# RWKV layer of a hybrid decoder: PSUM banks by size of product, key work in three staggered parts, bonus as four column tiles

## The chip, the cores and the metric

The kernel runs on one core of a Trainium2 chip. The metric is the device time of one execution in microseconds. TensorE (PE in the rows; PEld is its weight load) multiplies, VectorE (DVE) and ScalarE (ACT) work elementwise and empty PSUM, GpSimd (POOL) works elementwise in SBUF, SyncE (SP) issues most of the DMAs.

## The reference, cut to what matters

The model has two layers, one of sparse attention and one of RWKV-7 time mixing, each with a squared-ReLU MLP. The change is in the RWKV layer, for 256 tokens, 1024 features and 16 heads of 64:

```python
r, k, v = xr @ w_rkv[0], xk @ w_rkv[1], xv @ w_rkv[2]
decay = exp(-exp(w_log))
a = sigmoid(a0 + (xa @ a1) @ a2)
kk = k * k_k / |k * k_k|
kh = k * (1 + (a - 1) * k_a)
state = state * decay + (state @ -kk) * (kk * a) + v * kh     # one step per token
y = state @ r
y = groupnorm(y) * ln_w + ln_b + sum(r * kh * r_k) * v        # the last term is the bonus
out = (y * g) @ w_out
```

The kernel computes the recurrence in chunks of 64 tokens: inside a chunk the steps become products of matrices, with the inverse of a triangular matrix for each head and chunk, and a state goes from chunk to chunk.

## The kernel before

All weights come as chunks of 128 x 1024 (`wchunk`, from L227): SyncE loads a chunk into one of 4 buffers (wst), ScalarE rounds it (wh, L230), VectorE takes what the rounding left (wl, L232), with 5 buffers of each, and TensorE multiplies three times (L266 to L268). PSUM has two rings of four banks: `pmm` takes the next of the ring "mm", `pacc` the next of "acc". A tile waits until the tile that had its bank four allocations before is done with.

The RWKV layer runs, in the order of the program: receptance features (`feature_tile`, 8 of them), then for each of four pairs of feature tiles p and p + 4 the two key features (`keys_of`), and behind those of the next pair the key work of the pair (`key_pair`): the product pa for a with its tanh (th), the product pc with the exponentials E and Ei of the decay, the squares sq, on VectorE the products that fill AR and BK, the norms pn, the low blocks pL (LB and LO, the triangular parts, emptied by ScalarE at L986 to L989), on GpSimd F, kh in kk[:, 2:], the other half of BK, and r * kh (L1003), from which the bonus product pb (L1007) is made. Feature tiles use mm, everything in `key_pair` uses acc. Then the value product (`gemm_b`, 96 matmuls into acc) follows; its evacuation vt is also copied by DMA to VS. Then come, for chunks c, `products(c)` (pM, M; masked on GpSimd at L1073 for chunks 0 and 1, "late", and on VectorE at L1071 for 2 and 3), the gate products (pg), the key rows (pKB), and the gate steps on GpSimd (L1108 to L1111, on vt, bon, g and rowt).

The inverse stands behind that in the program: VectorE transposes and scales LB (L1123, L1124), then runs a loop of 31 steps, 116 instructions (L1130, L1133), transposes the result to T and TT (L1135, L1136); TensorE forms pU and pT (L1147, L1154) with copies T (L1149) and TT (L1156). A list of steps then runs over the chunks: Z right sides, Q solve with TT, S next state, M products, B key rows, Y output, N norm.

The order on every engine except SyncE is fixed when the kernel is built: a planner with a model of time goes through ready instructions, earlier ones of the program first. On the chip an engine keeps that order and waits. `issue_after(x)` puts the instructions that follow behind x on the engine of x; `first` (L1149) is such a mark for the chunks of the output weight. Larger tiles (`big`) take numbered slots from a free list and give them back with `done`.

Of the kernel before, what the change touches and what calls it, by code (L numbers as in the profile page):

```python
# [9 lines left out]
F32 = mybir.dt.float32  # L10
# [6 lines left out]
D = 1024  # L17
# [20 lines left out]
NSA_ORDER = ("K a0 h0 h1 l2 q0 q1 q2 q3 h2 G l3 T0 s0 a1 h3 s1 w0 H q4 q5 q6 q7 w1 "  # L38
             "C0 T1 s2 C1 s3 s4 P0 v0 v1 w2 P1 v2 s5 w3 s6 w4 v3 w5 v4 v5 w6 s7 v6 w7 v7").split()
LAG = 2  # L40
TAIL = 4
# [17 lines left out]
def _consts():  # L59
# [31 lines left out]
    mR = (s_ <= t_).astype(np.float32)  # L91
    parts["mmask"] = np.concatenate([mA, mR], 1).astype(np.float32)
    parts["par"] = np.stack([p < 64, p >= 64], 1).astype(np.float32)
    off, o = {}, 0
# [80 lines left out]
def trunk(ctx: ExitStack, tc: tile.TileContext, wb, x_in, wg, cw1k, cw1v, cw2, vecs_in, l1, w2, a2, g2, rows,  # L175
# [671 lines left out]
    def rwkv(inp):  # L847
        hn, dx, xrh, xrl, w2t, a2t, lo = inp
        with ExitStack() as es:
# [10 lines left out]

            rk2 = pool.tile([128, KT, 2], F32, name="rk2")
            P.tensor_tensor(rk2, cc("par")[:, None, :].to_broadcast([128, KT, 2]),
                            vec[:, V_RK * KT:V_RK * KT + KT][:, :, None].to_broadcast([128, KT, 2]), op=ALU.mult)
# [34 lines left out]
            def feature_tile(hT, lT, dst):  # L898

                wh, wl = wchunk("p (k c) -> p k c", k=8)  # L900
                p = pmm([128, S], "pa")
                for k in range(KT):
                    mm3(p, wh[:, k], wl[:, k], kt(hT, k), kt(lT, k), k == 0, k == KT - 1)
                act(dst, p, AF.Copy)
# [20 lines left out]
            bon = pool.tile([128, NT, H], F32, name="bon")  # L925
            bon4 = bon.rearrange("p t (i k s) -> p t i k s", i=2, k=4)
            F = pool.tile([128, NCH - 1, KT], F32, name="F")
# [17 lines left out]

            def key_pair(p, kk):

                ks_ = (p, p + 4)
                AR[p], BK[p] = big([128, 2, NCH, 2, C], f"AR{p}"), big([128, 2, NCH, 2, C], f"BK{p}")
                ar, bk = AR[p], BK[p]  # L950
                th = sm.tile([128, 2, S], F32, tag="th", bufs=2, name="th")
                th1 = sm.tile([128, 2, S], F32, tag="th1", bufs=2, name="th1")
                sq = sm.tile([128, 2, S], F32, tag="sq", bufs=2, name="sq")
                e_ = big([128, 2, NCH, C + 1], f"E{p}")
                Ei = big([128, 2, NCH, C + 1], f"Ei{p}")
                pa = pacc("pa2", [128, 2, S])
                for i, k in enumerate(ks_):
                    mm(pa[:, i], a2t[:, k * 128:(k + 1) * 128], aT, start=True, stop=True)
                for i, k in enumerate(ks_):
                    act(th[:, i], pa[:, i], AF.Tanh, scale=0.5, bias=hk[:, 0, k:k + 1])  # L960

                for i, k in enumerate(ks_):
                    pc = pacc("pc", [128, NT, 2, C + 1])
                    for t in range(NT):
                        mm(pc[:, t].rearrange("p c t -> p (c t)"), ld[t][:, k * 128:(k + 1) * 128], cen, start=True, stop=True)
                    act(e_[:, i], pc.rearrange("p a c t -> p (a c) t"), AF.Exp)
                    act(Ei[:, i], pc.rearrange("p a c t -> p (a c) t"), AF.Exp, scale=-1.0)
                for i, k in enumerate(ks_):
                    act(sq[:, i], kk[:, i], AF.Square, scale=vcol(V_KK, k))
                V.scalar_tensor_tensor(th1, th, 1.0, kk[:, :2], op0=ALU.add, op1=ALU.mult)  # L970
                for i, k in enumerate(ks_):
                    V.scalar_tensor_tensor(ar[:, i, :, 0], four(kk[:, i]), vcol(V_KK, k), e_[:, i, :, :C], op0=ALU.mult, op1=ALU.mult)
                    V.scalar_tensor_tensor(bk[:, i, :, i], four(th1[:, i]), vcol(V_KK, k), Ei[:, i, :, 1:], op0=ALU.mult, op1=ALU.mult)

                pn = pacc("pn", [128, NCH, 2])
                for c in range(NCH):
                    for i, k in enumerate(ks_):
                        mm(pn[rows_of(k), c], sq[:, i, c * C:(c + 1) * C], par, start=True, stop=True)
                pl = [pacc("pL", [128, NCH, C]) for _ in range(2)]
                for c in range(NCH):  # L980
                    for s in range(2):
                        for k in ks_:
                            mm(pl[s][rows_of(k), c], head(BK, k, s, c)[:, k // 4], head(AR, k, s, c)[:, 0], start=True, stop=True)
                for s in range(2):
                    lb, lo_ = [a.rearrange("p (c k s) t -> p c k s t", c=NCH, k=4)[:, :, p, s] for a in (LB, LO)]
                    act(lb, pl[s][:, :, :32], AF.Copy)  # L986
                    for r2 in r2s:
                        act(lb[r2], pl[s][r2, :, 32:], AF.Copy)
                    act(lo_, pl[s][:, :, 32:], AF.Copy)  # L989
                V.tensor_scalar(rn4[:, :, p], pn, 1e-24, -2.0, op0=ALU.max, op1=ALU.mult)  # L990
                for i, k in enumerate(ks_):
                    V.tensor_scalar(th[:, i], th[:, i], hk[:, 1, k:k + 1], hk[:, 2, k:k + 1], op0=ALU.mult, op1=ALU.add)
                P.tensor_tensor(kk[:, 2:], kk[:, :2], th, op=ALU.mult)
                for i in range(2):
                    P.tensor_tensor(bk[:, i, :, 1 - i], four(kk[:, 2 + i]), Ei[:, i, :, 1:], op=ALU.mult)

                    P.tensor_tensor(F[:, :, ks_[i]], e_[:, i, :NCH - 1, C], Ei[:, i, 1:, 0], op=ALU.mult)

                r2_ = pair_of(rr, p)
                V.tensor_tensor(ar.rearrange("p i c a t -> p (i c) a t")[:, :, 1], r2_.rearrange("p i (c t) -> p (i c) t", c=NCH),  # L1000
                                e_.rearrange("p i c t -> p (i c) t")[:, :, 1:], op=ALU.mult)

                P.tensor_tensor(kk[:, 2:], r2_, kk[:, 2:], op=ALU.mult)  # L1003
                pb = pacc("pb", [128, NT, 2, 2])
                for t in range(NT):
                    for i, k in enumerate(ks_):
                        mm(pb[:, t, i], kk[:, 2 + i, t * 128:(t + 1) * 128], rk2[:, k], start=True, stop=True)  # L1007
                act(bon4[:, :, :, p], pb, AF.Copy)
                done(e_, Ei, kk)


            kp = []

            def keys_of(p):
                kp.append(big([128, 4, S], f"kk{p}"))
                for i in range(2):
                    feature_tile(xkh, xkl, kp[p][:, i])
            keys_of(0)
            for p in range(1, 5):
                if p < 4:  # L1020
                    keys_of(p)
                if p == 3:
                    done(xkh, xkl)
                key_pair(p - 1, kp[p - 1])
            done(ld, a2t, rr)
            V.reciprocal(rn, rn)
            V.transpose(rnB, rn)

            Tb = big([128, 32, 32], "Tb")
            P.memset(Tb, 0.0)  # L1030
            dg = Tb.rearrange("p a b -> p (a b)")
            act(bass.AP(tensor=dg.tensor, offset=dg.offset, ap=[dg.ap[0], [33, 32]]), rnB, AF.Copy)

            sms.close()
            sm = es.enter_context(tc.tile_pool(name="rw2", bufs=1))
            Lb = big([128, 32, 32], "Lb")
            pd = big([128, 32, 32], "pd")
            T1 = big([128, 32, 32], "T1")
            vt = [big([128, D], f"vt{t}") for t in range(NT)]
            TT = sm.tile([128, 32, C], F32, name="TT")  # L1040
            for r2 in r2s:
                P.memset(TT[r2, :, :32], 0.0)
            VS = [big([128, H, DH], f"VS{c}") for c in range(NCH)]

# [6 lines left out]

            gemm_b(lambda k, sl: kt(xvh, k)[:, sl], lambda k, sl: kt(xvl, k)[:, sl], v_evac, D)
            done(xvh, xvl)


# [62 lines left out]
            key_rows(1)  # L1118
            gates(0)
            gates(1)  # L1120


            V.transpose(Lb.rearrange("p s t -> p t s"), LB.rearrange("p h t -> p t h"))  # L1123
            V.tensor_tensor(Lb, Lb, rnB[:, None, :].to_broadcast([128, 32, 32]), op=ALU.mult)  # L1124
            done(LB)
            for i in range(31):
                n, m_ = i + 1, 31 - i
# [15 lines left out]
            for bl in jb:  # L1143
# [4 lines left out]
                for p, r2 in zip(pU, r2s):  # L1148
                    first = act(T1[r2, bl], p[r2], AF.Copy)  # L1149
            for bl in jb:  # L1150
# [4 lines left out]
                for p, r1 in zip(pT, r1s):  # L1155
                    V.tensor_copy(TT[r1, bl, 32:], p[r1])  # L1156
            done(T1, LO)
# [115 lines left out]

            for o in "Z0 M2 Q0 S0 Z1 M3 B2 Q1 S1 Z2 Y0 Q2 S2 N0 Z3 Q3 Y1".split():
                if o[0] == "N":
# [79 lines left out]
```

## Time and profile before

| | us |
|---|---|
| median of 3 runs (767.73 to 768.32) | 767.97 |
| the profiled execution | 772.3 |
| its span | 770.5 |
| TensorE busy in the span | 732.2 (95%) |
| VectorE busy | 460.5 (60%) |
| ScalarE busy | 424.2 (55%) |
| GpSimd busy | 75.4 (10%) |
| mean granted clock of TensorE, as a share of 2.4 GHz | 0.969 |

Times in the rows are microseconds from the start of the span. Matmuls are pipelined: a row's time is longer than the distance to the next. The buffer numbers are left out of the names, so pa stands for the feature product and, at L958, for the product pa2, and th for th and th1; halves of an fp32 product are instructions of their own.

### The profile page before, as it was taken

To read this page: it belongs to the slowest core of one execution; us is meant where nothing else is said; L and a number is where in the kernel's file an instruction comes from. 1 tells how busy PE (TensorE), PEld (TensorE's weight loads), DVE (VectorE), ACT (ScalarE), POOL (GpSimd) and SP (SyncE) were. 2 spreads that over 40 slices of the span, in tenths; PEclk is the share of its full clock that TensorE was granted. 3 is DMA by queue.
4 is the path that set the end of the run, shared out by engine and by line. 5 is a ranking of instruction groups with operands and counts; after the bars stand their busy time and mean duration, and the time that the engine had idled before them with its cause. 6 is when DMAs were issued, how large, how long until landed. Compare 5 with 4: busy or idle time off the path is not lost. (4 is left out here: it accounts for less than half of the span.)

```text
span 770.5 us, 13414 instructions
## 1 busy us (share of the span) xinstructions
PE 732.2 (95%) x5292; PEld 627.9 (81%) x5292; DVE 460.5 (60%) x939; ACT 424.2 (55%) x830; POOL 75.4 (10%) x78
## 2 busy tenths in 40 slices
PE   7999999999999999999999669988899999999996
PEld 5876866789999899988899558678789899898995
DVE  5766798358455544578746469264765644555453
ACT  6626587347555655563657422565536655556562
POOL 1000000000000000001004550770110000000000
PEclk9999999999999999999999659979999999999999
DMA  8946200219655555680154102332214755555531
GB/s 286 324 137 249 81 31 6 81 55 316 187 188 188 189 184 180 214 273 1 62 185 138 55 0 90 92 103 83 87 51 137 234 186 187 188 191 191 189 114 54
DMA packets 32012, 111.50 MB, mean 145 GB/s; under 512 B 3629, under 2 KB 4141, under 8 KB 31950
## 3 DMA queue, kind: packets, MB, share of 16 engines
q1 hardware_dynamic: 30878, 108.94, 42.7%
q10 hardware_dynamic: 928, 1.19, 0.7%
q8 instruction: 41, 0.67, 0.4%
q0 software_dynamic: 144, 0.52, 0.2%
q14 instruction: 21, 0.17, 0.1%
HBM read 108.54 MB, written 1.05 MB: 142 GB/s over the span
## 5 line engine op out<-in xcount | busy, mean ns | idle before, releaser
L232 DVE TENSOR_TENSOR wl<-wst,wh 128x1024 fp32r<-128x1024 f32 x175 | 216.8, 1244 | 181.2 <-ACT wh L230 179.3
L230 ACT ACTIVATE wh<-wst 128x1024 fp32r<-128x1024 f32 x175 | 184.7, 1059 | 177.4 <-PE mu L267 77.8
L267 PE MATMUL mo<-wl,mqh 128*128 128x512 f32 x224 | 88.4, 395 | 0.0
L266 PE MATMUL mo<-wh,mqh 128*128 128x512 f32 x224 | 88.1, 395 | 0.0
L268 PE MATMUL mo<-wh,mql 128*128 128x512 f32 x224 | 87.2, 395 | 0.0
L266 PE MATMUL mu<-m0h,wh 128*128 128x256 f32 x256 | 72.5, 285 | 0.4 <-DVE m0l L304 0.4
L268 PE MATMUL mu<-m0h,wl 128*128 128x256 f32 x256 | 72.4, 284 | 0.0
L268 PE MATMUL mu<-m1h,wl 128*128 128x256 f32 x256 | 71.9, 282 | 0.0
L267 PE MATMUL mu<-m0l,wh 128*128 128x256 f32 x256 | 71.9, 282 | 0.0
L267 PE MATMUL mu<-m1l,wh 128*128 128x256 f32 x256 | 71.5, 280 | 0.0
L266 PE MATMUL mu<-m1h,wh 128*128 128x256 f32 x256 | 71.0, 281 | 0.0
L268 PEld LDWEIGHTS mo<-wh,mql 128*128 128x128 f32 x224 | 42.1, 188 | 9.9
L266 PEld LDWEIGHTS mu<-m0h,wh 128*128 128x128 f32 x256 | 48.2, 189 | 1.8 <-DVE m0l L304 0.6
L267 PEld LDWEIGHTS mu<-m0l,wh 128*128 128x128 f32 x256 | 48.4, 189 | 1.3 <-DVE m0l L304 0.2
L267 PEld LDWEIGHTS mu<-m1l,wh 128*128 128x128 f32 x256 | 48.1, 188 | 1.1
L266 PEld LDWEIGHTS mu<-m1h,wh 128*128 128x128 f32 x256 | 47.9, 188 | 1.2
L267 PEld LDWEIGHTS mo<-wl,mqh 128*128 128x128 f32 x224 | 42.2, 188 | 7.9
L266 PEld LDWEIGHTS mo<-wh,mqh 128*128 128x128 f32 x224 | 42.2, 188 | 7.7
L268 PEld LDWEIGHTS mu<-m0h,wl 128*128 128x128 f32 x256 | 48.1, 188 | 0.0
L268 PEld LDWEIGHTS mu<-m1h,wl 128*128 128x128 f32 x256 | 48.1, 188 | 0.0
L266 PE MATMUL acc<-wh,n0h 128*128 128x512 f32 x80 | 32.4, 411 | 0.0
L268 PE MATMUL acc<-wh,n0l 128*128 128x512 f32 x80 | 32.0, 402 | 0.0
(363 smaller groups left out, 1523.2 us busy)
## 6 DMA issues: line engine op xcount, KB each, us to landing
wst<-in_wb_dram SPq DMA_DIRECT2D x188, 512.0 KB, 4.3
w1t<-in_cw1k_dram SPq DMA_DIRECT2D x4, 512.0 KB, 6.8
w1t<-in_cw1v_dram SPq DMA_DIRECT2D x4, 512.0 KB, 8.2
x<-in_x_dram SPq DMA_DIRECT2D x4, 256.0 KB, 5.1
rowt<-in_rows_dram SPq DMA_DIRECT2D x2, 512.0 KB, 5.3
VS<-vt ACTq DMA_DIRECT2D x8, 128.0 KB, 5.1
out_dram<-xg SPq DMA_DIRECT2D x4, 256.0 KB, 2.2
g<-in_l_dram SPq DMA_DIRECT2D x2, 320.0 KB, 5.2
```

Of the source, the lines that this page charges most:

```text
L230: act(wh, st, AF.Copy)
L232: V.tensor_tensor(wl, st, wh.bitcast(F32), op=ALU.subtract)
L266: mm(o, lh, rh, start=first, stop=False)
L267: mm(o, lh, rl, start=False, stop=False)
L268: return mm(o, ll, rh, start=False, stop=last)
```

## The change

`KEY_ORDER` spreads the key work of a pair over three functions. `before_keys` (P) has what needs no key: pa, th, pc, E, Ei. `after_keys` (A) has the products with the key, the norms, and GpSimd's part. `low_blocks` (B) has pL and its evacuations. G is the pair's two key features. All of P, A and B use the ring mm, and the features use acc, as the values do. In A each BK comes ahead of its AR, and th, kk and the rest of BK come ahead of the low blocks.

The bonus leaves the pairs. The four kk tiles are kept; behind the values 8 matmuls of 256 columns, each with 32 columns of weights, write four groups of 32 partitions of one bank, and two matmuls with a constant "stk" bring them to tokens by heads. Chunk 2's products move from the list of steps to between the gate steps, masked on GpSimd ("late"). T1 takes its slot after LB is given back. `first` becomes the last copy of TT, on VectorE, in place of the last copy of T1 on ScalarE. In the list M2 goes, and Q0 follows Z0 directly.

```diff
+KEY_ORDER = "P0 G0 P1 G1 A0 P2 G2 A1 B0 P3 G3 A2 B1 A3 B2 B3".split()
...
+            rki = pool.tile([128, KT, 32], F32, name="rki")
+            P.memset(rki, 0.0)
...
             def feature_tile(hT, lT, dst):
...
-                p = pmm([128, S], "pa")
+                p = pacc("pa", [128, S])
...
-            def key_pair(p, kk):
+            def before_keys(p):
...
-                pa = pacc("pa2", [128, 2, S])
+                pa = pmm([128, 2, S], "pa2")
...
-                    pc = pacc("pc", [128, NT, 2, C + 1])
+                    pc = pmm([128, NT, 2, C + 1], "pc")
...
+                return th, e_, Ei
+
+            def after_keys(p, kk, th, e_, Ei):
...
                 V.scalar_tensor_tensor(th1, th, 1.0, kk[:, :2], op0=ALU.add, op1=ALU.mult)
                 for i, k in enumerate(ks_):
+                    V.scalar_tensor_tensor(bk[:, i, :, i], four(th1[:, i]), vcol(V_KK, k), Ei[:, i, :, 1:], op0=ALU.mult, op1=ALU.mult)
                     V.scalar_tensor_tensor(ar[:, i, :, 0], four(kk[:, i]), vcol(V_KK, k), e_[:, i, :, :C], op0=ALU.mult, op1=ALU.mult)
-                    V.scalar_tensor_tensor(bk[:, i, :, i], four(th1[:, i]), vcol(V_KK, k), Ei[:, i, :, 1:], op0=ALU.mult, op1=ALU.mult)
-
-                pn = pacc("pn", [128, NCH, 2])
+                    act(sq[:, i], kk[:, i], AF.Square, scale=vcol(V_KK, k))
+
+                pn = pmm([128, NCH, 2], "pn")
...
+            def low_blocks(p):
+                pl = [pmm([128, NCH, C], "pL") for _ in range(2)]
...
-                pb = pacc("pb", [128, NT, 2, 2])
-                for t in range(NT):
-                    for i, k in enumerate(ks_):
-                        mm(pb[:, t, i], kk[:, 2 + i, t * 128:(t + 1) * 128], rk2[:, k], start=True, stop=True)
-                act(bon4[:, :, :, p], pb, AF.Copy)
...
+            values = gemm_parts(lambda k, sl: kt(xvh, k)[:, sl], lambda k, sl: kt(xvl, k)[:, sl], v_evac, D)
...
+            for _ in values:
+                pass
             done(xvh, xvl)
+
+            pb = pacc("pb", [128, S])
+            for i in range(2):
+                for j in range(4):
+                    mm(pb[32 * j:32 * j + 32], rki[:, 4 * i + j], kp[j][:, 2 + i], start=i == 0, stop=i == 1)
+            bonT = sm.tile([128, S], F32, name="bonT")
+            act(bonT, pb, AF.Copy)
+            pb = pacc("pbT", [128, NT, H])
+            for t in range(NT):
+                mm(pb[:, t], bonT[:, t * 128:(t + 1) * 128], cc("stk"), start=True, stop=True)
+            act(bon, pb, AF.Copy)
+            done(kp)
...
             gates(0)
+            Ms[2] = products(2, True)
             gates(1)
...
             done(LB)
+            T1 = big([128, 32, 32], "T1")
...
-                    first = act(T1[r2, bl], p[r2], AF.Copy)
+                    act(T1[r2, bl], p[r2], AF.Copy)
...
-                    V.tensor_copy(TT[r1, bl, 32:], p[r1])
+                    first = V.tensor_copy(TT[r1, bl, 32:], p[r1])
...
-            for o in "Z0 M2 Q0 S0 Z1 M3 B2 Q1 S1 Z2 Y0 Q2 S2 N0 Z3 Q3 Y1".split():
+            for o in "Z0 Q0 M3 B2 S0 Z1 Q1 S1 Z2 Y0 Q2 S2 N0 Z3 Q3 Y1".split():
```

## Rows read from the trace of the kernel before

**Rows 1.** Windows by stage: length, busy us by engine, granted clock, DMA share, GB/s.

```profile
395.40:425.80 30.40, 30.40 (x294) 29.29 (x292) 18.89 (x26) 19.93 (x44) 10.06 (x10) 1.00 0.43 140
425.80:458.30 32.50, 18.00 (x175) 15.86 (x174) 15.97 (x27) 12.77 (x42) 19.52 (x24) 0.61 0.10 33
458.30:483.40 25.10, 25.10 (x97) 19.82 (x97) 24.41 (x118) 5.16 (x7) 1.04 (x2) 0.89 0.23 69
465.00:480.00 15.00, 15.00 (x66) 12.06 (x65) 14.72 (x61) 3.32 (x4) 0.00 (x0) 1.00 0.38 115
483.40:511.00 27.60, 25.84 (x423) 17.96 (x422) 10.91 (x8) 18.06 (x29) 24.98 (x11) 1.00 0.32 97
511.00:557.80 46.80, 41.12 (x682) 36.74 (x682) 27.54 (x46) 24.44 (x56) 8.16 (x5) 0.85 0.27 92
```

**Rows 2.** Waits of TensorE, 425.8 to 458.3: us in total, times, longest.

```profile
PE pb L1007 <- POOL kk L1003: 9.0, 3, 4.4
PE pL L983 <- DVE BK L973: 5.5, 3, 2.6
```

**Rows 3.** Timeline of TensorE, small products at the full clock: start, us, instruction.

```profile
406.84 1.02 PE L958 MATMUL pa<-wa,a2t 128*128 128x256 f32 x4
407.70 1.05 PE L965 MATMUL pc<-cst,ld 128*128 128x130 f32 x8
408.69 0.63 PE L978 MATMUL pn<-cst,sq 128*64 128x2 f32 x16
...
415.48 0.68 PE L983 MATMUL pL<-AR,BK 64*64 64x64 f32 x28
...
417.86 0.95 PE L1007 MATMUL pb<-rk,kk 128*128 128x2 f32 x8
```

**Rows 4.** Timeline of VectorE: key work of the last pair, inverse.

```profile
446.50 0.69 DVE L970 SCALAR_TENSOR_TENSOR th<-th,kk 128x512 f32<-128x512 f32 x1 [7.33 <-ACT th L960]
...
448.94 0.69 DVE L1000 TENSOR_TENSOR AR<-rr,E 128x512 f32<-128x512 f32 x1
449.55 1.48 DVE L973 SCALAR_TENSOR_TENSOR BK<-th,vec,Ei 128x256 f32<-128x256 f32 x1
...
454.15 1.94 DVE L1123 STREAM_TRANSPOSE Lb<-LB 128x1024 f32<-128x1024 f32 x1 [2.40 <-ACT LB L988]
...
457.72 0.19 DVE L1130 TENSOR_TENSOR pd<-Tb,Lb 128x31 f32<-128x31 f32 x1
...
464.92 1.22 DVE L232 TENSOR_TENSOR wl<-wst,wh 128x1024 fp32r<-128x1024 f32 x1
...
478.44 0.43 DVE L1130 TENSOR_TENSOR pd<-Tb,Lb 128x96 f32<-128x96 f32 x2
...
482.96 0.29 DVE L1133 TENSOR_TENSOR Tb<-Tb,pd 128x15 f32<-128x15 f32 x2
```

**Rows 5.** Timeline of GpSimd: last pair, gate steps, masks.

```profile
448.71 2.04 POOL L993 TENSOR_TENSOR kk<-kk,th 128x512 f32<-128x512 f32 x1 [0.62 <-DVE th L992]
...
485.95 1.90 POOL L1108 TENSOR_TENSOR vt<-vt,bon 128x1024 f32<-128x1024 f32 x1 [26.36 <-DMA VS<-vt]
...
492.10 4.64 POOL L1073 TENSOR_TENSOR M<-M,cst 128x1024 f32<-128x1024 f32 x2
...
503.63 5.67 POOL L1073 TENSOR_TENSOR M<-M,cst 128x1024 f32<-128x1024 f32 x2
509.26 5.66 POOL L1111 TENSOR_TENSOR g<-g,rowt 128x1024 f32<-128x1024 f32 x2
```

**Rows 6.** Timeline of VectorE beside GpSimd's masks.

```profile
507.11 0.69 DVE L1071 TENSOR_TENSOR M<-pM,cst 128x512 f32<-128x512 f32 x1
507.72 2.66 DVE L232 TENSOR_TENSOR wl<-wst,wh 128x1024 fp32r<-128x1024 f32 x1
```

**Rows 7.** Timeline of TensorE: the first solve, and products on two column tiles.

```profile
511.03 0.33 PE L1195 MATMUL pQ<-Zt,TT 64*64 64x64 f32 x2 [1.62 <-DVE TT L1156]
...
533.33 1.15 PE L1223 MATMUL pY<-VS,M 128*64 128x64 f32 x24
```

More of the change, by code (lines that the diff above doesn't have):

```diff
@@ L92, in _consts @@
     parts["mmask"] = np.concatenate([mA, mR], 1).astype(np.float32)
+    parts["stk"] = (p[:, None] % 32 == np.arange(16)[None, :]).astype(np.float32)
     parts["par"] = np.stack([p < 64, p >= 64], 1).astype(np.float32)
@@ L859, in rwkv @@
             P.tensor_scalar(hk[:, 2], vec[:, V_KA * KT:V_KA * KT + KT], -0.5, 1.0, op0=ALU.mult, op1=ALU.add)
-            rk2 = pool.tile([128, KT, 2], F32, name="rk2")
-            P.tensor_tensor(rk2, cc("par")[:, None, :].to_broadcast([128, KT, 2]),
+            rki = pool.tile([128, KT, 32], F32, name="rki")
+            P.memset(rki, 0.0)
+            rkf = rki.rearrange("p a b -> p (a b)")
+            P.tensor_tensor(bass.AP(tensor=rkf.tensor, offset=rkf.offset, ap=[rkf.ap[0], [34, KT], [1, 2]]),
+                            cc("par")[:, None, :].to_broadcast([128, KT, 2]),
                             vec[:, V_RK * KT:V_RK * KT + KT][:, :, None].to_broadcast([128, KT, 2]), op=ALU.mult)
@@ L925, in rwkv @@
             bon = pool.tile([128, NT, H], F32, name="bon")
-            bon4 = bon.rearrange("p t (i k s) -> p t i k s", i=2, k=4)
             F = pool.tile([128, NCH - 1, KT], F32, name="F")
@@ L944, in rwkv @@
             LO = big([128, 32, 32], "LO")
-            def key_pair(p, kk):
+            def before_keys(p):
                 ks_ = (p, p + 4)
[L949 to L955, printed above, removed]
-                pa = pacc("pa2", [128, 2, S])
+                th = sm.tile([128, 2, S], F32, tag="th", bufs=3, name="th")
+                e_, Ei = big([128, 2, NCH, C + 1], f"E{p}"), big([128, 2, NCH, C + 1], f"Ei{p}")
+                pa = pmm([128, 2, S], "pa2")
                 for i, k in enumerate(ks_):
@@ L967, in key_pair @@
                     act(Ei[:, i], pc.rearrange("p a c t -> p (a c) t"), AF.Exp, scale=-1.0)
-                for i, k in enumerate(ks_):
-                    act(sq[:, i], kk[:, i], AF.Square, scale=vcol(V_KK, k))
+                return th, e_, Ei
+            def after_keys(p, kk, th, e_, Ei):
+                ks_ = (p, p + 4)
+                AR[p], BK[p] = big([128, 2, NCH, 2, C], f"AR{p}"), big([128, 2, NCH, 2, C], f"BK{p}")
+                ar, bk = AR[p], BK[p]
+                th1 = sm.tile([128, 2, S], F32, tag="th1", bufs=1, name="th1")
+                sq = sm.tile([128, 2, S], F32, tag="sq", bufs=2, name="sq")
                 V.scalar_tensor_tensor(th1, th, 1.0, kk[:, :2], op0=ALU.add, op1=ALU.mult)
                 for i, k in enumerate(ks_):
+                    V.scalar_tensor_tensor(bk[:, i, :, i], four(th1[:, i]), vcol(V_KK, k), Ei[:, i, :, 1:], op0=ALU.mult, op1=ALU.mult)
                     V.scalar_tensor_tensor(ar[:, i, :, 0], four(kk[:, i]), vcol(V_KK, k), e_[:, i, :, :C], op0=ALU.mult, op1=ALU.mult)
-                    V.scalar_tensor_tensor(bk[:, i, :, i], four(th1[:, i]), vcol(V_KK, k), Ei[:, i, :, 1:], op0=ALU.mult, op1=ALU.mult)
-                pn = pacc("pn", [128, NCH, 2])
+                    act(sq[:, i], kk[:, i], AF.Square, scale=vcol(V_KK, k))
+                pn = pmm([128, NCH, 2], "pn")
                 for c in range(NCH):
@@ L978, in key_pair @@
                         mm(pn[rows_of(k), c], sq[:, i, c * C:(c + 1) * C], par, start=True, stop=True)
[L979 to L989, printed above, removed]
                 V.tensor_scalar(rn4[:, :, p], pn, 1e-24, -2.0, op0=ALU.max, op1=ALU.mult)
@@ L1003, in key_pair @@
                 P.tensor_tensor(kk[:, 2:], r2_, kk[:, 2:], op=ALU.mult)
-                pb = pacc("pb", [128, NT, 2, 2])
-                for t in range(NT):
-                    for i, k in enumerate(ks_):
-                        mm(pb[:, t, i], kk[:, 2 + i, t * 128:(t + 1) * 128], rk2[:, k], start=True, stop=True)
-                act(bon4[:, :, :, p], pb, AF.Copy)
-                done(e_, Ei, kk)
-            kp = []
+                done(e_, Ei)
+            def low_blocks(p):
+                pl = [pmm([128, NCH, C], "pL") for _ in range(2)]
+                for c in range(NCH):
+                    for s in range(2):
+                        for k in (p, p + 4):
+                            mm(pl[s][rows_of(k), c], head(BK, k, s, c)[:, k // 4], head(AR, k, s, c)[:, 0], start=True, stop=True)
+                for s in range(2):
+                    lb, lo_ = [a.rearrange("p (c k s) t -> p c k s t", c=NCH, k=4)[:, :, p, s] for a in (LB, LO)]
+                    act(lb, pl[s][:, :, :32], AF.Copy)
+                    for r2 in r2s:
+                        act(lb[r2], pl[s][r2, :, 32:], AF.Copy)
+                    act(lo_, pl[s][:, :, 32:], AF.Copy)
+            kp, pre = [], []
             def keys_of(p):
@@ L1017, in keys_of, with v_evac @@
                     feature_tile(xkh, xkl, kp[p][:, i])
-            keys_of(0)
-            for p in range(1, 5):
-                if p < 4:
-                    keys_of(p)
[L1022 to L1025, printed above, removed]
+            def v_evac(cb, t, p):
+                act(vt[t][:, cb * 512:(cb + 1) * 512], p, AF.Copy)
+                for c in range(2):
+                    nc.scalar.dma_start(VS[2 * t + c][rows_of(4 - 4 * cb), 8 * cb:8 * cb + 8].rearrange("p h d -> p (h d)"),
+                                        vt[t][64 * c:64 * c + 64, cb * 512:(cb + 1) * 512])
+                    P.memset(VS[2 * t + c][rows_of(4 * cb), 8 * cb:8 * cb + 8], 0.0)
+            values = gemm_parts(lambda k, sl: kt(xvh, k)[:, sl], lambda k, sl: kt(xvl, k)[:, sl], v_evac, D)
+            for o in KEY_ORDER:
+                p = int(o[1:] or 0)
+                if o[0] == "P":
+                    pre.append(before_keys(p))
+                    if p == 3:
+                        done(ld, a2t)
+                elif o[0] == "G":
+                    keys_of(p)
+                    if p == 3:
+                        done(xkh, xkl)
+                elif o[0] == "A":
+                    after_keys(p, kp[p], *pre[p])
+                    if p == 3:
+                        done(rr)
+                elif o[0] == "B":
+                    low_blocks(p)
+                elif o[0] == "V":
+                    next(values)
             V.reciprocal(rn, rn)
@@ L1037, in rwkv @@
             pd = big([128, 32, 32], "pd")
-            T1 = big([128, 32, 32], "T1")
             vt = [big([128, D], f"vt{t}") for t in range(NT)]
@@ L1043, in rwkv @@
             VS = [big([128, H, DH], f"VS{c}") for c in range(NCH)]
-            def v_evac(cb, t, p):
-                act(vt[t][:, cb * 512:(cb + 1) * 512], p, AF.Copy)
-                for c in range(2):
-                    nc.scalar.dma_start(VS[2 * t + c][rows_of(4 - 4 * cb), 8 * cb:8 * cb + 8].rearrange("p h d -> p (h d)"),
-                                        vt[t][64 * c:64 * c + 64, cb * 512:(cb + 1) * 512])
-                    P.memset(VS[2 * t + c][rows_of(4 * cb), 8 * cb:8 * cb + 8], 0.0)
-            gemm_b(lambda k, sl: kt(xvh, k)[:, sl], lambda k, sl: kt(xvl, k)[:, sl], v_evac, D)
-            done(xvh, xvl)
+            for _ in values:
+                pass
+            done(xvh, xvl)
+            pb = pacc("pb", [128, S])
[9 more added lines that the diff above has]
+            done(kp)
             mmask = cc("mmask")
```

## The prediction

> **What bounds the kernel now.** I read the page first (where TensorE is not full), then a table of stages around the key work of the RWKV layer, then each engine's timeline there. TensorE is full and at 2.4 GHz from 395.4 to 425.8 us. From 425.8 to 458.3 it has 18.0 us of busy time in 32.5 us, at a mean granted clock of 0.61; then the value product runs without a gap to 483.4, its start still at the lower level [rows 1]. The reader should see that this hole isn't want of work: the value product needs nothing of what the hole computes, and its matmuls begin only behind the last bonus product. TensorE stands before the bonus (pb) for GpSimd's kk and before the low blocks (pL) for VectorE's BK [rows 2]; being in order, it can't pass them. Meanwhile a second chain ends: LB is complete at 454.15, VectorE inverts the triangles from 457.72 to 483.25, and the products of chunks 0 and 1 and the gates (483.4 to 511.0) hide what follows the inverse [rows 1, 4]. So TensorE's order sets the time up to 511, and the inverse has some 15 us of slack. After 511 the chain over chunks runs with holes, at a clock of 0.85 [rows 1].
>
> **The front part.** Dense products take the acc banks and small ones the mm banks, so the value accumulators no longer wait for a bank of the last pair. The last feature product ends at 425.8 now. Two more preparations move ahead of it: 0.86 us for pa and 0.99 for pc each, 3.7 together; the bonus of pair 0 (0.8) and a few low blocks (0.2) move behind it [rows 3]. That gives 428.5. Behind it lie two pn (0.6 each), three pL (0.7 each) and some 0.5 for changes between forms, 3.8 us, which the values may surround; the 96 value matmuls take 22.4 us at the full clock (15.0 us hold 64 to 66 of them) [rows 1, 3]. The values end at 454.7 instead of 483.4: 28.7 us. I take the clock as full, as in 395.4 to 425.8, where the same mixture ran without a hole [rows 1]. The bound below is no gain at all (the values stay behind the pairs), the bound above 32.5 - 10 = 22.5 for the hole, 2.6 for the slow start and 3.3 for the four old bonuses, 28.4. The two ways agree. ScalarE's 32 evacuations of low blocks and the roundings of value weights stay as many; they bunch behind 428.5, which I price below.
>
> **The bonus.** Four times 8 instructions (0.8 us each time, 3.2) leave; 16 instructions of 256 columns in four column tiles come, and two small products with two evacuations. At 0.22 us (pa: four in 0.86) the 16 cost 3.5 if one follows the other, 0.9 if four run side by side. The nearest row with column tiles, pY in two halves of 64, issues 24 instructions of 64 columns in 1.07 us, 0.045 each, against 0.054 for a quarter of pa [rows 3, 7]; so I take 3.0, and 1.0 more for the rest. The Trainium skill (TensorEngine Tiling (Array Packing), Key Properties) says that tiles operate independently and can run matmuls in parallel; by it the 16 would cost 0.9, two microseconds less.
>
> **Behind the values.** Bonus, products of chunk 0, gate products, key rows, products of chunk 1 and now those of chunk 2 follow. In 483.4 to 511.0 that work, with the inverse's two small products and Z0, was 25.8 us busy [rows 1]. Shifted by 28.7, TensorE alone would reach Q0 near 482 to 484. Chunk 2's 32 products leave the gap between Z0 and Q0, with their four masks on VectorE; GpSimd gets two masks of 2.3 us [rows 5]. The new mark on the output weights binds VectorE's roundings to come after TT's copies: of the 2.6 us rounding that held Q0 at 511.03, about 2 us go [rows 6, 7].
>
> **The inverse becomes the bound.** Its start: the last key tile is evacuated near 429.3; th1 and four products take 2.2 us (446.50 to 449.55 is 3.05 with two other steps between), low blocks 0.9, then evacuation: 3.1 us lay between the last BK (451.03) and Lb (454.15) at the half clock. I take 3.0, and up to 2 for two other pairs' evacuations ahead on ScalarE. Lb and its scaling take 3.6. The loop starts at 440 to 441, not 457.7. It lasted 25.5 us with three weight roundings inside, 1.14 each, so 22.1 net [rows 4]; one or two fall inside now. It would end near 464.5, 19 us earlier.
>
> But GpSimd is at work by then. Now its gates begin at 485.95, 2.5 us behind the values, when the loop is over [rows 5]. After the change they begin 2.5 us behind 454.7, or when the bonus is out: 458 to 460. The trace shows what two inputs in SBUF do on both engines. GpSimd's kk product at 448.71 waits for VectorE's L1000 (to 449.63); then VectorE's L973, 0.48 by itself, takes 1.48, to 451.03, just behind GpSimd's end at 450.75. The rounding at 507.72 ends 1.1 us (its own length) behind the end of the second mask at 509.30; the mask at 507.11, which reads PSUM, isn't slowed [rows 4 to 6]. So one blocks the other for a whole instruction, and turns are taken. The loop's steps are such products, of 0.13 to 0.2 us at the end: from 478.44 to 483.25 there are 34 [rows 4]. GpSimd's are 1.9 to 2.35 us. The Trainium skill (SBUF — State Buffer, Who interferes with whom) speaks against the change here: the pair of ports is held for the whole instruction and the other engine fully blocks. It doesn't say who is next, and no row shows a stream of short instructions against a stream of long ones.
>
> At 459 some 5 us of the loop are left, about 34 instructions. GpSimd's queue is eight gate steps (two of 1.9, six of 2.35) and six masks of 2.32, 31.8 us, and it waits for nothing of the inverse. With two short ones per long one (L1000 slipped past the waiting kk, so one to three), 34 need all 14: the loop ends at 459 + 31.8 + some 3 = 493 to 495; with three, or with 20 instructions left, 10 to 11 long ones pass: 485 to 487. With none, 464.5. I take 493. Behind it T is transposed (2.0), then come the first half of pU, ScalarE's copies, half of pT and the TT copies, 8 us with TensorE at its lower level after standing (estimate: 64 instructions of either at 0.02 us, doubled, two copies of 0.6 and of 0.7, and handovers). Q0 starts at 503 against 511.0: 8 us.
>
> **After Q0.** Chunk 2's products are gone from ahead of it, and gates and masks are done, so that no output weight waits for their buffers. Against that, rounding comes later on VectorE, and the clock starts low, as it does now (0.85 over the stage). Of 46.8 us with 5.7 idle I take 4 as gained; bounds 0 and 7 [rows 1]. Everything later only shifts.
>
> **The sum.** 8 + 4 = 12 us of the profiled execution, whose span is 770.5 (772.3 with what lies around it). The median of the runs shown is 767.97, so 756.
>
> **Rivals.** *The loop keeps its place* (chance 0.18): it ends before GpSimd starts, or VectorE's back-to-back steps hardly let it in. Then TensorE binds, Q0 at 482 to 484, 27 to 29 us and 4 behind: 735 to 737. For it: three engines' estimates must miss by only 5 us. Against: my start of GpSimd is tied to the same 428.5. *A part of GpSimd's queue passes* (0.20): 10 to 20 loop instructions are left, five to eight long ones pass, the loop ends at 476 to 483, Q0 is at 486 to 493: 739 to 746. *Slower* (0.05): ScalarE's bunched evacuations of low blocks hold LB until 444, so the loop starts at 448; at 459 some 70 instructions are left, all 14 long ones pass with one short one each (to 494), and 56 more take 9 us. Then T is late, Q0 is at 513 and the chain starts on a low clock: 770. It decides once the loop ends later than 501, where Q0 passes 511, and nothing is gained behind it. *The values don't move* (0.04): the order fixed at build leaves them behind the last pair; then only the bonus and Q0's wait count, 766.5 to 768.
>
> **How the numbers follow.** The forecast, 756 (750 to 764), has 0.53. The range from 733 to 765 leaves out about 0.1; it takes in the free loop below. About 0.2% (1.5 us) is what this measurement can tell from no change: faster 0.91, same 0.04, slower 0.05.
>
> **What would show it.** Value matmuls between low blocks from about 429, clock 1.0 there, last one near 455; the loop's start near 440; from 459 loop steps on VectorE of over 2 us beside GpSimd's gates and masks; a hole in TensorE of 10 to 20 us ahead of Q0. Loop steps of 0.25 us beside a busy GpSimd, or a GpSimd that starts behind the loop, would make this wrong on the fast side.

## The result: slower by 0.8%

| | before | after |
|---|---|---|
| median, us | 768.12 (767.73 to 768.32) | 774.37 (773.51 to 775.75) |
| ratio to before, 95% interval | | 1.0084 (1.0066 to 1.0101) |
| the profiled execution; its span | 772.3; 770.5 | 773.79; 772.0 |
| inverse's loop, first to last instruction | 457.72 to 483.25 | 442.97 to 485.51 |
| TensorE's Q0 | 511.03 | 514.02 |
| first matmul of the output projection (roa) | 557.81 | 558.38 |

The forecast was 756, faster. Windows by stage, of the changed kernel (length, then busy time and instructions of PE, PEld, DVE, ACT, POOL, then granted clock, DMA share, GB/s), answer to [rows 1]:

```profile
395.40:425.80 30.40, 30.40 (x296) 29.72 (x295) 25.48 (x35) 22.58 (x53) 18.44 (x19) 1.00 0.43 140
425.80:455.20 29.40, 29.40 (x234) 23.70 (x233) 26.38 (x68) 12.81 (x35) 16.45 (x17) 0.94 0.33 95
455.20:470.40 15.20, 14.70 (x85) 7.53 (x84) 15.10 (x20) 6.22 (x12) 12.48 (x6) 1.00 0.29 75
470.40:487.50 17.10, 0.09 (x1) 0.00 (x0) 16.89 (x50) 0.00 (x0) 7.83 (x4) 0.61 0.16 57
487.50:514.00 26.50, 26.50 (x366) 24.05 (x366) 7.55 (x7) 14.29 (x22) 11.62 (x5) 0.50 0.02 3
514.00:558.30 44.30, 36.88 (x675) 32.24 (x674) 24.97 (x42) 24.79 (x55) 3.96 (x3) 0.95 0.32 107
```

The old hole is gone: TensorE is busy through all of 425.8 to 455.2, and the values are out 28 us earlier, as intended. But then it stands for 17.1 us with one instruction, and runs 26.5 us fully busy at the lower of its two levels (0.50, 1.2 GHz). Those two stages eat the whole gain. What filled them shows on GpSimd and VectorE. First GpSimd's timeline of the changed kernel (start, us, instruction, and in brackets the idle time before), then VectorE's; they answer to [rows 4, 5]:

```profile
457.92 3.90 POOL L1134 TENSOR_TENSOR vt<-vt,bon 128x1024 f32<-128x1024 f32 x2 [15.09 <-ACT bon L1078]
461.79 2.38 POOL L1135 TENSOR_TENSOR vt<-vt,rowt 128x1024 f32<-128x1024 f32 x1
464.13 4.73 POOL L1099 TENSOR_TENSOR M<-M,cst 128x1024 f32<-128x1024 f32 x2
468.82 2.39 POOL L1135 TENSOR_TENSOR vt<-vt,rowt 128x1024 f32<-128x1024 f32 x1
471.18 4.71 POOL L1136 TENSOR_TENSOR vt<-vt,g 128x1024 f32<-128x1024 f32 x2
475.86 2.37 POOL L1137 TENSOR_TENSOR g<-g,rowt 128x1024 f32<-128x1024 f32 x1
495.77 4.66 POOL L1099 TENSOR_TENSOR M<-M,cst 128x1024 f32<-128x1024 f32 x2 [17.54 <-ACT M L1095]
```

```profile
457.47 0.49 DVE L1158 TENSOR_TENSOR pd<-Tb,Lb 128x126 f32<-128x126 f32 x2
457.87 2.19 DVE L1161 TENSOR_TENSOR Tb<-Tb,pd 128x126 f32<-128x126 f32 x2
459.99 4.33 DVE L1158 TENSOR_TENSOR pd<-Tb,Lb 128x117 f32<-128x117 f32 x2
464.24 4.77 DVE L1161 TENSOR_TENSOR Tb<-Tb,pd 128x117 f32<-128x117 f32 x2
469.05 4.65 DVE L1158 TENSOR_TENSOR pd<-Tb,Lb 128x120 f32<-128x120 f32 x2
473.62 4.75 DVE L1161 TENSOR_TENSOR Tb<-Tb,pd 128x120 f32<-128x120 f32 x2
478.29 0.46 DVE L1158 TENSOR_TENSOR pd<-Tb,Lb 128x110 f32<-128x110 f32 x2
...
485.22 0.29 DVE L1161 TENSOR_TENSOR Tb<-Tb,pd 128x15 f32<-128x15 f32 x2
```

Two loop instructions take 0.46 to 0.49 us alone and 4.3 to 4.8 us beside GpSimd. In the 20.3 us of GpSimd's nine steps VectorE gets 11 instructions through, the ones at either edge included: one per GpSimd step, and at once 0.2 us each when GpSimd stops at 478.2. Then TensorE's and ScalarE's timelines of the same kernel:

```profile
469.34 1.16 PE L1091 MATMUL pM<-AR,BK 64*128 64x128 f32 x8
487.50 0.74 PE L1175 MATMUL pU<-T,LO 32*32 32x32 f32 x20 [17.01 <-DVE T L1163]
488.18 3.09 PE L1091 MATMUL pM<-AR,BK 64*128 64x128 f32 x16
...
514.02 1.12 PE L1223 MATMUL pQ<-Zt,TT 64*64 64x64 f32 x16
```

```profile
469.01 0.60 ACT L1129 ACTIVATE KB<-pKB 128x512 f32<-128x512 f32 x1
489.46 2.13 ACT L1166 ACTIVATE TT<-TT 32x1024 f32<-32x1024 f32 x2 [19.85 <-DVE TT L1164]
491.61 0.60 ACT L1129 ACTIVATE KB<-pKB 128x512 f32<-128x512 f32 x1
```

TensorE had most products of chunks 1 and 2 to do, whose inputs were long there (e2 below does them all by 476). But the order fixed at build puts pU ahead of them, and ScalarE's copy of TT ahead of their evacuations. So both engines stand until T is there, and do that work behind it.

### The profile page after: what moved, and what is told of

Its sections match the earlier page's. It is cut to its first block, busy times and chain, and to the rows that moved or that the text cites. A ratio compares the mean times of both kernels' runs of the same rounds, so it can differ in the third digit from the quotient of the medians.

```text
span 772.0 us, 13391 instructions
## 1 busy us (share of the span) xinstructions
PE 730.9 (95%) x5280; PEld 626.7 (81%) x5280; DVE 479.3 (62%) x935; ACT 425.3 (55%) x832; POOL 83.0 (11%) x81
## 4 chain that ended last, share of the span: by engine, by line
PE 85%; DVE 10%; ACT 2%; issue 1%; DMA 1%; SPq 0%; POOLq 0%; POOL 0%; DVEq 0%; ACTq 0%
PE mu L269 8%; PE mu L268 8%; PE mu L270 8%; PE mo L270 7%; PE mo L268 7%; PE mo L269 7%; DVE Tb L1161 3%; PE acc L268 3%; DVE pd L1158 2%; PE acc L269 2%; PE acc L270 2%; PE pa L269 2%; PE pa L270 2%; PE pa L268 2%; PE S L628 2%; PE pM L1091 2%
```

## The experiments

Two theories. **L**: GpSimd's steps hold the loop, one loop instruction passing between two of them; that costs some 20 us. **O**: the order of TensorE and ScalarE behind the values leaves the hole empty, and the lower clock follows.

| run | median, us | ratio to before (95%) | loop ends | first pU | Q0 |
|---|---|---|---|---|---|
| c0_before | 768.49 | 0.9991 (0.9975 to 1.0007) | | | 510.73 |
| e1_pool_behind | 756.92 | 0.9838 (0.9804 to 0.9871) | 466.5 | 468.61 | 496.24 |
| e2_pe_order | 770.01 | 1.0013 (0.9985 to 1.0040) | 496.6 | 498.57 | 510.41 |
| e3_both | 748.08 | 0.9746 (0.9692 to 0.9800) | 466.4 | 474.69 | 489.57 |
| e4_four_two_input | 800.39 | 1.0403 (1.0373 to 1.0433) | 501.4 | 503.39 | 544.23 |
| e5_copies | 800.84 | 1.0413 (1.0377 to 1.0449) | 500.7 | 502.71 | 541.92 |
| e6_act_order | 748.72 | 0.9735 (0.9700 to 0.9769) | 468.3 | 470.34 | 491.41 |
| e7_pool_seq | 750.35 | 0.9747 (0.9713 to 0.9780) | 467.1 | 477.21 | 489.77 |
| e8_hold | 746.80 | 0.9722 (0.9691 to 0.9753) | 466.5 | 475.00 | 484.53 |
| e9_hold_c1 | 749.67 | 0.9729 (0.9697 to 0.9760) | 466.6 | 471.39 | 484.09 |
| e10_m2_list | 768.10 | 0.9988 (0.9973 to 1.0003) | 486.4 | 488.52 | 512.20 |
| e11_four_gates_behind | 789.49 | 1.0270 (1.0256 to 1.0284) | 488.7 | 490.75 | 530.98 |

**The kernel before, again.**

> The kernel before, unchanged, as a measure of its own repeatability and of where its profiled execution (span 770.5 us) lies 4 us above its timed runs. Expected: 768 us, ratio 1.000 within 0.2%; the output projection starts at 554 to 558 us.

It came out so. The front agrees with the first trace to 0.3 us (Q0 510.73), but roa starts at 555.86 and not at 557.81: the execution profiled first took 1.7 us more between Q0 and roa. So of a difference of a few us between two traces, 2 can be scatter between executions.

**GpSimd behind the loop** (the masks are taken out of `products`):

```diff
-            gates(0)
             Ms[2] = products(2, True)
-            gates(1)
...
+            behind = P.tensor_copy(inv_end, Tb[:, :, 31])
+            with tc.issue_after(behind.ins):
+                for c in range(3):
+                    masks(c)
+                for t in range(NT):
+                    gates(t)
```

> The changed kernel, with GpSimd's gate steps and masks of all three chunks moved behind the end of the inverse's loop. Theory L (two-input products on GpSimd hold the loop): the loop, alone, runs its natural length and ends at 466 to 468 us instead of 485.5, TensorE's 17 us wait for T's transpose is gone, the clock stays at its upper level, Q0 starts at 483 to 488 instead of 514, time 745 to 755 us. Theory O (only the order of TensorE's and ScalarE's queues matters): pU and the copy of TT still stand ahead of M1 and M2, Q0 stays within 4 us of 514, time 770 to 775.

The loop ended as L had it, at 466.5, 19 us earlier than in the changed kernel. But Q0 is at 496.24, not at 483 to 488, the time is 2 us above the range, and the clock fell. TensorE and ScalarE of this run, and TensorE's window behind:

```profile
466.77 0.60 ACT L1131 ACTIVATE KB<-pKB 128x512 f32<-128x512 f32 x1
470.58 2.13 ACT L1173 ACTIVATE TT<-TT 32x1024 f32<-32x1024 f32 x2 [3.22 <-DVE TT L1171]
472.74 0.60 ACT L1131 ACTIVATE KB<-pKB 128x512 f32<-128x512 f32 x1
```

```profile
473.39 2.07 PE L1091 MATMUL pM<-AR,BK 64*128 64x128 f32 x8 [1.96 <-ACT KB L1131]
```

```profile
475.00:505.00 30.00, 30.00 (x355) 0.50 0.23 72
```

ScalarE's copy of TT holds an evacuation of key rows, TensorE waits 1.96 us for the bank, and from there it runs 30 us at the lower level though it is never idle. L is right on the loop; on the time O has a share.

**TensorE's and ScalarE's order alone** (GpSimd as in the changed kernel):

```diff
+                        with tc.issue_after(last_pe[0].ins), tc.issue_after(last_pe[1].ins):
                             mm(p[r2, j - bl.start], LO[r1, j], T1[r1, j], start=True, stop=True)
...
+                with tc.issue_after(last_act[0].ins), tc.issue_after(last_act[1].ins):
                     act(TT[r1, :, :32], TT[r1, :, 32:], AF.Copy)
```

`last_pe` are the last product of chunk 2 and the last key row, `last_act` their evacuations.

> The changed kernel with GpSimd's work where it is, but TensorE issues pU only behind the last product of chunk 2 and the last key rows, and ScalarE copies TT only behind their evacuations. Theory O: the products fill the hole at the upper clock, while masks of chunks 1 and 2 fall into the loop too and lengthen it; loop ends at 495 to 497, Q0 starts at 505 to 508 instead of 514, time 765 to 768 us. Theory L alone (only the loop's length matters, the order is without effect): loop ends 10 us later and everything behind it too, Q0 at 514 to 520, 774 us or more.

The loop's end and the products came as O had it; Q0 and the time came 2 us later than its ranges. TensorE of this run:

```profile
473.15 2.82 PE L1094 MATMUL pM<-AR,BK 64*128 64x128 f32 x32 [0.77 <-ACT M L1098]
498.57 3.63 PE L1180 MATMUL pU<-T,LO 32*32 32x32 f32 x128 [22.60 <-DVE T L1166]
```

The products of chunks 0 to 2 are done by 476, so Q0 follows pU by 12 us instead of 26.5. But now the masks of chunks 1 and 2 are ready early and fall into the loop as well: in the 32.2 us of 14 GpSimd steps VectorE gets 16 instructions through, and TensorE has a hole of 22.6 us. This cure alone feeds the other cause, L.

**Both edits together.**

> Both edits: GpSimd's gates and masks behind the loop, and pU behind the products. If the loop ends near 467, as theory L has it, TensorE has products to issue until about 480 anyway, and the order costs and gains little: Q0 at 482 to 488, 742 to 753 us, within 3 us of the run with GpSimd's move alone. Theory O alone: 765 to 768, as with the order alone.

748.08, 20 us below before: with both edits the change is worth that. No run puts the same edits on the kernel before, so how much of it belongs to the front part alone stays open. It is 9 us faster than GpSimd's move alone, not within 3, since the order also kept the clock up (the next run shows it). What binds next, on ScalarE and TensorE:

```profile
488.06 1.06 ACT L232 ACTIVATE wh<-wst 128x1024 fp32r<-128x1024 f32 x1 [8.20 <-DMA wst<-in_wb_dram]
```

```profile
489.57 1.51 PE L1235 MATMUL pQ<-Zt,TT 64*64 64x64 f32 x16 [5.27 <-ACT Zt L1227]
```

**ScalarE's order alone, GpSimd behind the loop.** As e1, with the second half of the diff of e2 only.

> The changed kernel with GpSimd's work behind the loop, and with ScalarE's copies of TT behind the evacuations of chunk 2's products and key rows, while TensorE's pU stays interleaved with products of chunks 1 and 2. It tells apart why the clock fell at 470 us in the run with GpSimd's move alone. If TensorE's 2 us wait there for ScalarE's key rows starts it, the clock stays at its upper level, Q0 starts at 483 to 488 and the time is 745 to 750 us. If the mixture of forms itself keeps it low, the lower level lasts from about 470 to 505 as in that run, Q0 starts at 494 to 498 and the time is 754 to 758 us.

The first case, on clock and time: 748.72 us, and TensorE is at 1.00 and busy 18.35 of 19 us in 466 to 485, with pU still among the products. TensorE's window (length, busy time and instructions, clock, DMA share, GB/s):

```profile
466.00:485.00 19.00, 18.35 (x393) 1.00 0.19 58
```

Q0 came at 491.41, later than 483 to 488, for ScalarE's wait of 7.7 us for a weight, as in e3. So of O it is the place of the TT copy on ScalarE that costs 8 us, by TensorE's wait and the clock behind it; TensorE's own order is harmless once T is early.

**The price of the hold, and the slack of the inverse**, in the kernel before:

```diff
...
+                if i == 10:
+                    mark = P.tensor_copy(mark_t, Tb[:, :, i])
+                    with tc.issue_after(mark.ins):
+                        for _ in range(4):
+                            P.tensor_tensor(scr[0], scr[0], scr[0], op=ALU.mult)
```

> The kernel before, with four additional GpSimd products of a scratch tile with itself (128 x 1024, two inputs in SBUF, results not used), issued behind the tenth step of the inverse's loop, where GpSimd is idle. Theory L: each stops the loop for its own length, 2.3 to 2.4 us, and one loop instruction passes between two of them; the loop ends 9.4 us later, near 492.7 instead of 483.25. If the inverse has the 15 us of slack that the prediction gives it, Q0 stays near 511 and the time at 768 us. If the order of TensorE fixed at build, with pU at 486 right behind chunk 0's products, leaves no slack (theory O), TensorE stands on pU for 9 us and the time is 776 to 779 us, more if the clock falls. Without a lock the loop ends at 483 and the time is 768.

800 us, more than any figure expected. GpSimd's four products:

```profile
464.21 8.80 POOL L1136 TENSOR_TENSOR scr<-scr 128x1024 f32<-128x1024 f32 x4
```

In these 8.80 us VectorE got 6 instructions through, the edges included: one each. The loop, thus late, was still running at 485.44 when the gates began, as they do in before, met them too, and ended at 501.4. TensorE:

```profile
503.39 1.17 PE L1156 MATMUL pU<-T,LO 32*32 32x32 f32 x36 [17.77 <-DVE T L1144]
504.49 2.08 PE L1090 MATMUL pg<-gw,gT 128*128 128x512 f32 x2
```

The gate products take 2.08 us a pair there, 1.12 at the full clock. The 15 us of slack that the prediction gave the inverse didn't exist.

**The same with the gates behind the loop**, to take the second meeting out:

```diff
-            gates(0)
-            gates(1)
...
+            behind = P.tensor_copy(inv_end, Tb[:, :, 31])
+            with tc.issue_after(behind.ins):
+                for c in range(2):
+                    masks(c)
+                for t in range(NT):
+                    gates(t)
```

> The kernel before with the four additional GpSimd products beside the loop, and its gate steps and masks behind the loop's end. With the gates in their place the run took 800 us: the loop, 9 us late, met the gates and lost 9 more, TensorE stood 17.8 us on pU, and the clock fell behind that. If the second meeting is a cause of its own, the loop ends at 491 to 493 (before: 483.25, with the gates in place: 501.4), TensorE stands 8 to 9 us on pU, and the time is 777 us if the clock stays up, 785 to 793 if it falls. If the four products alone explain it, the time stays near 800.

789.49, in the range for a falling clock: the second meeting is a cause of its own, worth some 10 us. The loop ended at 488.7 and not at 491 to 493, and the wait was shorter than 8 us, in part because in this execution the loop also began earlier (455.56 against 457.72 in before). What is left comes from the four products. TensorE's wait and its window behind it:

```profile
490.75 1.17 PE L1163 MATMUL pU<-T,LO 32*32 32x32 f32 x36 [5.73 <-DVE T L1151]
```

```profile
490.75:530.00 39.25, 39.25 (x372) 24.99 (x373) 9.06 (x8) 15.24 (x23) 26.21 (x12) 0.50 0.17 55
```

pU starts 4.8 us later than in before (485.96), and what lies between it and Q0 takes 40.2 us instead of 25.1, fully busy at the lower level. 4.8 + 15.1 = 19.9 us, and Q0 is 20 us later (530.98 against 511.03). TensorE has the same products in the same order there as in before, and no idle time, so the move of the gates adds no wait of its own. A wait of 5.7 us cost 20.

**Copies instead of products.** As e4, with eight times `P.tensor_copy(scr[0], scr[0])`.

> As the run with four two-input products, but with eight GpSimd copies of a 128 x 1024 tile (one input in SBUF) at the same place. If only two-input instructions exclude one another, the loop keeps its length, ends at 483 to 484, and the time is 768 us. If any GpSimd instruction holds VectorE's two-input steps, the loop ends later by the length of eight copies (8 to 16 us), and the time is 776 to 785 us.

Copies hold the loop as well. GpSimd and VectorE of this run:

```profile
463.80 9.23 POOL L1136 COPY scr<-scr 128x1024 f32<-128x1024 f32 x6
```

```profile
466.16 1.31 DVE L1142 TENSOR_TENSOR Tb<-Tb,pd 128x120 f32<-128x120 f32 x2
```

A single copy has a row of 1.04 us, in this row one takes 1.54, and two loop instructions (1.3 us, 0.47 alone) pass per copy; 13 VectorE instructions passed in 9.3 us. The planner put two copies among the gate steps, so six met the middle of the loop. They made it late enough that eight of its last twelve instructions met the gates and those two copies (485.3 to 500.2), and the time is that of e4, above both cases expected.

**Chunk 2's products back in the list** (the changed kernel, with M2 between Z0 and Q0, masked on VectorE):

```diff
-            Ms[2] = products(2, True)
...
-            for o in "Z0 Q0 M3 B2 S0 Z1 Q1 S1 Z2 Y0 Q2 S2 N0 Z3 Q3 Y1".split():
+            for o in "Z0 M2 Q0 M3 B2 S0 Z1 Q1 S1 Z2 Y0 Q2 S2 N0 Z3 Q3 Y1".split():
```

> The changed kernel with chunk 2's products back between Z0 and Q0, masked on VectorE, as before the change. It tells what that part of the change is worth. As predicted (part of the 4 us behind Q0): 774 + 2 = 776 us. If chunk 2's products, which stand ahead of pT at the lower clock, delay T more than they save behind it: 769 to 773 us. If it does not matter: 774 us, ratio within 0.3%.

768.10, a little below the second case: this part of the change costs 6 us as it stands. From pU to Q0 it is 23.7 us instead of 26.5, and from Q0 to roa 40.2 instead of 44.4. The mechanism of the second case isn't what the trace shows: the planner puts chunk 2's products ahead of Q0 here too, and TensorE has no fewer matmuls from pU to Q0 (378 against 366), but its mean granted clock there is 0.57 instead of 0.50. Why it rises sooner, and why the stretch behind Q0 is shorter, stays open.

**Toward a better one.** First GpSimd's 14 steps in a chosen order, on top of both edits:

```diff
+            for step in steps:
+                with tc.issue_after(behind.ins):
+                    behind = step()
```

> The kernel with both edits, and GpSimd's 14 steps behind the loop put in one order: bonus and the addition of the first row vector for both token tiles, then the masks of chunks 0, 1, 2, then the two gate products. The first row vector's buffer comes free near 475 instead of 484.5, so the output weight that ScalarE waited for (8.2 us, to 488.06, with Zt queued behind it) lands near 479. Theory: ScalarE's wait was what held Q0 at 489.57; Q0 starts at 484 to 486, the 5 us hole and the clock's dip behind it are gone, time 740 to 744 us. If the mask of chunk 0, now done at 480 instead of 471.5, is late instead, Q0 stays at 487 to 490 and the time at 746 to 750.

The weight came earlier (rounded at 479.95), but no gain, 750.35. ScalarE now had that rounding ahead of its copies of T, TensorE stood 0.9 us before pT, and its granted clock was 0.67 in 485 to 495; that the one caused the other isn't shown. The mask of chunk 0, the second case's suspect, is not waited for. Also the front was 2.2 us later in this execution than in e3 (below). Then the third weight held behind Q0's evacuations instead:

```diff
-hold=[(first.ins,)] * 2 + [(first.ins, st_done[0].ins)]
+hold=[(first.ins,)] * 2 + [(first.ins, st_done[0].ins, vals_done[0].ins)]
```

> The kernel with both edits (GpSimd's work behind the loop; pU and the copy of TT behind the products), and ScalarE's rounding of the third output weight placed behind its copies of Q0's values. In the run with both edits, ScalarE stood 8.2 us on that weight's load with Zt queued behind it, and TensorE 5.27 us before Q0. If that wait is what holds Q0, Q0 starts at 484 to 486 instead of 489.57, the clock does not fall behind it, and the time is 738 to 743 us. If the wait only moves (to VectorE's roundings or to the output projection's weights), Q0 starts earlier but the time stays at 745 to 749 us.

Q0 is at 484.53, 5 us earlier, and the time 746.8 (743.5 to 751.2): the wait only moved. TensorE and VectorE of this run:

```profile
489.56 0.69 PE L1264 MATMUL pY<-VS,M 128*64 128x64 f32 x4 [2.61 <-DVE M L1100]
```

```profile
483.71 5.19 DVE L234 TENSOR_TENSOR wl<-wst,wh 128x1024 fp32r<-128x1024 f32 x2
488.83 1.27 DVE L1100 TENSOR_TENSOR M<-pM,cst 128x512 f32<-128x512 f32 x2
```

Two roundings that take turns with GpSimd's steps (5.19 us instead of 2.4) stand ahead of chunk 3's mask. Last, pU and the copy of TT freed from chunk 2's products:

> As the run with the third weight held, but pU and the copy of TT only behind chunk 1's products and key rows, not behind chunk 2's. T is there at 468.5 and chunk 1's products end near 470, so pU may start some 4 us earlier. If T's own chain (pU, pT and their copies) is what Q0 then waits for, Q0 starts 2 to 4 us earlier, and the time is 735 to 741 us. If Q0 waits for Zt, or if the interleaved order brings back TensorE's short waits and the lower clock, no gain: 740 to 750 us.

No gain: 749.67, with a ratio of 0.9729 against 0.9722. pU starts 3.6 us earlier (471.39 against 475.00), but the last copy of TT ends only 0.2 us earlier (482.9 against 483.1), so this run doesn't make T early. Q0 starts at 484.09 instead of 484.53, and in both runs without idle time of TensorE ahead of it: it waits for TensorE's own work. The five runs from 746.8 to 750.4 can't be ranked by these numbers; all beat both kernels: before by 2.5 to 2.8%, and the changed one by 3.3 to 3.6% (their ratios to before over its 1.0084). The smallest edit among them is e6.

## Why the prediction was wrong, step by step

**The front part was right.** The values start at 429.8 (429 forecast), the last value matmul ends near 455.2 (454.7), in one stretch with the low blocks between. That is 28.2 us earlier; the 28.7 of the forecast lay above the bound of 28.4 that it set itself. The loop starts at 442.97 (440 to 441) with two roundings inside. GpSimd starts at 457.92 (458 to 460).

**The bonus was mis-sized**: 16 instructions in 1.07 us where 3.0 were taken.

```profile
455.23 1.07 PE L1072 MATMUL pb<-kk,rki 128*32 128x256 f32 x16
```

The Trainium skill (TensorEngine Tiling (Array Packing), Key Properties) says that tiles run in parallel. The trace comes close to the 0.9 us that followed from it.

**The meeting of loop and gates was right in kind, off in three sizes** that pull against each other. When GpSimd starts, the loop has some 54 instructions left, not 34, and one of them passes per GpSimd step, not two. But GpSimd stopped after nine steps, not fourteen, as its next mask waited for ScalarE's M (17.54 us idle). The loop ended at 485.5, earlier than the 493 forecast; that it came so near is partly luck.

**The step that failed is "Behind the values"** with the tail set on it. It took the products of chunks 0 to 2 as work that TensorE does as soon as the values are out, and 10 us from the loop's end to Q0. TensorE and ScalarE keep the order of the build, in which pU and the copy of TT lie among those products. So 17 us of the time gained were spent standing, the products followed at half the clock, and the tail was 28.5 us: Q0 at 514.02 instead of 503. e2 shows the tail without them, 13.8 us, still 4 more than the 10 taken. The hole of 10 to 20 us that the prediction named as a sign did come (17.0 us), but ahead of that work and not behind it. The prediction did state that engines keep the order and wait, and did foresee a low clock there, for 8 us; it asked of each instruction when its inputs are ready, not what stands ahead of it. The trace of before had said so: pU starts 2.7 us behind the loop's end and long before the products of chunk 1 are done:

```profile
485.96 0.76 PE L1147 MATMUL pU<-T,LO 32*32 32x32 f32 x36
...
498.53 2.05 PE L1065 MATMUL pM<-AR,BK 64*128 64x128 f32 x24
```

So "the inverse has some 15 us of slack" was wrong too, by e11: 5.7 us of wait cost 20.

**After Q0** 4 us were taken as gained. From Q0 to roa it is 44.4 us, against 46.8 in the trace that the sum was made on, and 45.1 in its repetition. Chunk 2's products, which the prediction took as done long before Q0, still ran in the stretch ahead of it (498.9 to 507.4), and that part of the change lost 6 us as it stands (e10).

**The sum by the traces**: Q0 3.0 us later (3.3 against the repetition), 2.4 (0.8) gained behind it, 0.9 lost behind roa: 1.5 us (3.4), where the medians say 6.3. The rest isn't in these executions; the prediction's step from span to median carried that scatter unseen. Of the rivals, "slower" had the right lock and the wrong place: it took a loop that ends later than 501, and 485.5 was late enough.

## What to carry to other kernels

When work is moved ahead, read the fixed order of every in-order engine between it and the next consumer: an instruction with ready inputs behind one that waits is as late as that one. A loop of short VectorE instructions must be kept apart from GpSimd's large ones by an explicit order, not by the time at which they happen to start; before missed its meeting by 2.7 us, and any change that moves either side can fall off that edge. Price a hole on TensorE with the clock that follows it (5.7 us became 20), and try two cures together where one alone can feed the other cause.

## What the runs showed of the hardware

- GpSimd and the loop's two-input steps on VectorE took strict turns: one instruction of either for one of the other where GpSimd has two inputs in SBUF (VectorE's count with the edges: 11 beside 9 GpSimd steps, 16 beside 14, 6 beside 4), and two of VectorE for each one-input copy (e5, the six copies beside the middle of the loop). Why two there, no run shows. The Trainium skill (SBUF — State Buffer, Who interferes with whom) gives GpSimd no read port but the one shared with VectorE. The copies agree with that: one input is enough to block.
- Behind a wait, the lower level (0.50) lasted on while TensorE was fully busy in the rows: 26.5 us behind 17.0 us of waiting in the changed kernel, at least 30 behind 2.0 in e1, 39 behind 5.7 in e11. What ends it, the runs don't show.
- It also came without any idle time before it. In the changed kernel and in e7 the first values ran at the lower level to 433.3, right behind pn and pL; in the other seven runs with the same order of work there, e3 among them, they did not. TensorE of the changed kernel and of e3:

```profile
429.26 0.63 PE L984 MATMUL pn<-cst,sq 128*64 128x2 f32 x8
429.82 0.69 PE L268 MATMUL acc<-wh,xvh 128*128 128x512 f32 x1
430.31 0.63 PE L269 MATMUL acc<-wl,xvh 128*128 128x512 f32 x1
```

```profile
428.99 0.49 PE L268 MATMUL acc<-wh,xvh 128*128 128x512 f32 x1
429.32 0.40 PE L269 MATMUL acc<-wl,xvh 128*128 128x512 f32 x1
```

  The first twelve value matmuls, up to the next pL, take 4.5 us there (429.82 to 434.36) and 3.0 in e3 (428.99 to 431.99). In all, the same front ends within 2.4 us in these runs (the bonus starts at 452.86 to 455.23).
